# Matmul operands at many 16-byte steps modulo 256, and every second paired unit's products in halves of 256 tokens, in a two-layer encoder trunk

## The chip, the cores and the metric

The kernel runs on one core of a Trainium2 chip, in one launch. The metric is the device time of that core in microseconds: three runs of the kernel before, and one further execution taken by the hardware profiler.

## The reference

Two sequences of 512 tokens (prompt and sample), width 1024, pass through the same two layers with the same parameters. Layer 1 is differential attention with 8 heads, layer 2 bidirectional retention with 8 heads; each layer projects into a width of 2048, gates the mixer's output and projects back:

```python
def diff_attention(h, w_in, lq1, lk1, lq2, lk2, subln_g, w_out, lambda_init):
    proj = h @ w_in
    q, k, v, gate = jnp.split(proj, [DA_QK_WIDTH, 2 * DA_QK_WIDTH, 2 * DA_QK_WIDTH + D_INNER], axis=-1)
    ...  # rotary on q and k; per head two score maps, softmax, a = p0 - lam * p1, a @ v
    o = rms_norm(o, subln_g, SUBLN_EPS) * (1.0 - lambda_init)
    o = o.reshape(B, S, D_INNER) * jax.nn.silu(gate)
    return o @ w_out

def trunk(x, norm_g, ...):
    for i in range(DEPTH):            # DEPTH = 2
        h = rms_norm(x, norm_g[i], NORM_EPS)
        x = x + (diff_attention if i % 2 == 0 else bidir_retention)(h, ...)
    return rms_norm(x, final_norm_g, NORM_EPS)
```

All of it is float32. The matmuls read their operands as float32r, and a product is made of three: high part by high part, high by low, low by high.

## The kernel before

**Stages.** Input norm and the first projection; attention with its output projection; the second projection; retention with its output projection; the final norm. The two sequences are the two columns of a 2 x 2 block product, and each projection is done with seven block products (P1 to P7) in place of eight: the sums and differences of weight blocks are made for each unit, those of token blocks once for each layer.

**Token operands.** `make_b` writes, for each of seven names (B11, B21, T1, T2, B22, T3, T4) and four parts k of the contraction, a buffer `[128, 2, 512]`: high and low part of 512 tokens. `slot(n, ...)` gives each its place: 18 places in one large tile `arena`, and tiles of their own (`b12`, `b13`, `b20` to `b27`) for the others. The same places later hold q, k, v, the attention weights `aT` and the mixer's output `oT`. A place starts in the arena at `32 + at * 1024 + shift` elements of four bytes; `shift` is 0, 16 or 32 elements, so that the places stand at three steps of 64 bytes modulo 256.

**Units.** A `Unit` is 256 columns of an input projection. A *paired* unit (q, k or gate; 24 in layer 1 and 16 in layer 2) computes transposed: the weights are the stationary operand, 128 columns at a time, and 512 tokens are the moving operand, 12 matmuls for each product (4 parts by 3 passes, line 573). A *wide* unit (v; 4 in each layer) has the tokens stationary, 128 at a time, and 256 weight columns moving, 48 matmuls for each product (line 580). `prep` splits a product's weights into high and low parts in buffers `ws`, a ring of `WS_BUFS = 7`. `evac` empties the PSUM banks: `c` copies on ScalarE, sums into `e` on VectorE (line 610). The ring of `e` has 8 places.

**Other matmuls.** Line 1007 is attention's scores, line 1059 attention times v, line 1160 retention's scores, line 1178 retention times v, line 824 the output projection (`oT` stationary, `ws` moving), lines 755, 946 and 1043 transposes.

**Order.** Every operation is recorded with a cost and its dependencies in a `Plan`, which then lays them out engine by engine; a ring's place is taken again when all who used it are done. TensorE's operations keep the recorded order within a window of 24. A product of a paired unit is one operation of cost 2.79, whatever matmuls it issues.

Of the kernel before, what the change touches and what calls it, by code (L numbers as in the profile page):

```python
# [10 lines left out]
F32R = mybir.dt.float32r  # L11
# [4 lines left out]
P = 128  # L16
S = 512
D = 1024
KT = D // P
NT = S // P  # L20
# [10 lines left out]
PASSES = ((0, 0), (0, 1), (1, 0))  # L31
WS_BUFS = 7
# [208 lines left out]
def trunk_kernel(  # L241
# [7 lines left out]
    nc = tc.nc  # L249
    xs = (x_prompt, x_sample)  # L250
    ys = (y_prompt, y_sample)
    plan = Plan()

    sm = ctx.enter_context(tc.tile_pool(name="sm", bufs=1))
    cp = ctx.enter_context(tc.tile_pool(name="cp", bufs=1))
    ar = ctx.enter_context(tc.tile_pool(name="ar", bufs=1))
# [10 lines left out]
    def view(pool, tag, i, size, shape, dt=F32):  # L267


        if size % 16 and pool in (cp, wk):  # L270
            pool = sm
        if (tag, i) not in places:
            places[tag, i] = pool.tile([P, size], F32, tag=f"{tag}{i}", name=f"{tag}_{i}", bufs=1)
        n = math.prod(shape[1:])
        t = places[tag, i][0:shape[0], 0:n]
        if dt != F32:
            t = t.bitcast(dt)
        if len(shape) == 3:
            t = t.rearrange("p (a b) -> p a b", a=shape[1])
        elif len(shape) == 4:  # L280
            t = t.rearrange("p (a b c) -> p a b c", a=shape[1], b=shape[2])
        return t

    def work(tag, shape, bufs, dt=F32, name=None):
        size = SIZE.get(tag, shape[1])
        return Buf(plan, tag, bufs, lambda i: view(wk, tag, i, size, shape, dt))

    arena = ar.tile([P, 18 * 1024 + 80], F32R, tag="arena", name="arena")

    def slot(n, shape, dt=F32R, shift=0):  # L290

        size = math.prod(shape[1:])
        at = None if n in (12, 13) or n >= 20 else n if n < 12 else n - 2
        if at is None:
            assert not shift
            cnt[0] += 1
            label = f"b_{cnt[0]}"
            return Buf(plan, f"b{n}", 1, lambda i: cp.tile(shape, dt, tag=f"b{n}", name=label))  # L300
        assert dt == F32R
        lo = 32 + at * 1024 + shift

        def make(i):
            t = arena[:, lo:lo + size]
            return t.rearrange("p (a b) -> p a b", a=shape[1]) if len(shape) == 3 else t
        b = Buf(plan, f"b{n}", 1, make)
        b.also = Buf(plan, f"edge{at + 1 if shift else at}", 1, None)
        return b

    def const(shape, tag, dt=F32):
        return Buf(plan, tag, 1, lambda i: view(cp, tag, i, math.prod(shape[1:]), shape, dt))

    def ws_t(shape):
        return work("ws", shape, WS_BUFS, F32R)

    def raw_t(shape):
        return work("raw", shape, 4)
# [5 lines left out]
        return work("c", [P, S], 4, name=name)  # L324

    def e_t(name="e"):
        return work("e", [P, S], 8, name=name)

    def m_t(name="m"):
        return work("m", [P, S], 4, name=name)  # L330
# [9 lines left out]
    def bank(tag, name=None):  # L340
        return Buf(plan, tag, BUFS[tag], lambda i: view(pj if tag == "pj" else sc, tag, i, S, [P, S]))
# [31 lines left out]
    def pe(cost, fn, r, w):  # L373
        plan.op("PE", cost, fn, r, w)

    def dma(out, in_, r, w, kb, eng=None):

        q = eng or nc.sync
        plan.op("SP" if eng is None else "ACT", 0.5, lambda: q.dma_start(out(), in_()), r, w, lands=2.0 + kb / 200.0,
                kb=kb, load=any(isinstance(k[0] if isinstance(k, tuple) else k, Buf) for k in w))  # L380
# [109 lines left out]
            yield  # L490


    class Unit:
        def __init__(self, w, c0, kind, done, view=None):


            self.w, self.c0, self.kind, self.done = w, c0, kind, done
            self.view = view or (lambda r, i: r[:, :, i * P:(i + 1) * P])
            self.wide = kind == "wide"
            self.n_ws = 2 if self.wide else 1  # L500
            self.early = None
            self.ops, self.x, self.s = {}, {}, {}
            self.banks = {}

# [55 lines left out]
        def product(self, op):  # L560
            which = BANK_OF[op]
            n_banks = 2 if self.wide else 1
            opens = op in OPENS
            if opens:
                self.banks[which] = [bank(dict(x="pj", z="sc", y="o")[which], which) for _ in range(n_banks)]
            a, b = self.ops.pop(op), B_OF[op]
            bt = [Bop[b, k] for k in range(4)]
            reads = [q[1] for q in a] + bt

            def pair(ps):  # L570
                for k in range(4):
                    for i, (u, v) in enumerate(PASSES):
                        nc.tensor.matmul(  # L573
                            ps.t, a[u][0]()[:, k, :], bt[k][:, v, :], start=(opens and k == 0 and i == 0),
                            stop=(k == 3 and i == 2), skip_group_check=True)

            def wide(ps, t):
                for k in range(4):
                    for i, (u, v) in enumerate(PASSES):
                        nc.tensor.matmul(  # L580
                            ps[:, (t % 2) * 256:(t % 2) * 256 + 256], bt[k][:, v, t * P:(t + 1) * P],
                            a[u][0]()[:, k, :], start=(opens and t % 2 == 0 and k == 0 and i == 0),
                            stop=(k == 3 and i == 2), skip_group_check=True)

            if not self.wide:
                ps = self.banks[which][0]
                pe(2.79, lambda: pair(ps), reads, [ps])
                return
            for t in range(NT):
                ps = self.banks[which][t // 2]  # L590
                pe(1.43, lambda ps=ps, t=t: wide(ps, t), reads, [ps])
# [172 lines left out]
        lo_of(256, lambda: oT[1][:, :, tok], lambda: og.t, lambda: oT[0][:, :, tok], [og, (oT[0], t)], [(oT[1], t)])  # L764

    def new_oT(g):
        return [slot(16 + 2 * g + a, [P, 2, S], F32R, 32) for a in range(2)]

    def load_qk(src, i, shift):
        t = slot(i, [P, 2, S], F32R, shift)  # L770
        dma(lambda: t.t.bitcast(F32), lambda: src[0][src[1]], [src[0]], [t], 512)
        return t

    def load_v(src, i):
        out = []
        for a in range(2):
            t = slot(i + a, [P, NT, 256], F32R, 16)
            dma(lambda a=a, t=t: t.t.bitcast(F32), lambda a=a: src[a].rearrange("p (t e) -> p t e", t=NT),
                [src], [t], 512)
            out.append(t)  # L780
        return out

    def load_sg(src):
        t = os_t(F32, "sg")
        dma(lambda: t.t, lambda: src[:], [src], [t], 512)
        return t
# [68 lines left out]
    qk_d = {}  # L855
# [132 lines left out]
    qk, vt, sg, oT = {}, {}, {}, {}  # L988
    st = [{} for _ in tiles]

    def fetch1(h, g):
        for j in range(2):
            for which in range(2):
                qk[h, g, j, which] = load_qk((qk_d[0, which, h, g], j), 4 * which + 2 * g + j, 16 * which)
        vt[h, g] = load_v(v_d[0, h, g], 8 + 2 * g)
        sg[h, g] = load_sg(g_d[0, h, g])

# [39 lines left out]
    def transp(i):  # L1037
        p = st[i]['p']
        tp = bank("tp", "tpa")

        def fn():
            for j in range(NT):
                nc.tensor.transpose(tp[:, j * P:(j + 1) * P], p[:, 0, j * P:(j + 1) * P], ident.t)  # L1043
        pe(0.44, fn, [p, ident], [tp])
        aT = slot(14 + i % 2, [P, 2, S], F32R, 32)
        hi_of(S, lambda: aT[:, 0, :], lambda: tp.t, [tp], [(aT, 0)])
        lo_of(S, lambda: aT[:, 1, :], lambda: tp.t, lambda: aT[:, 0, :], [tp, (aT, 0)], [(aT, 1)])
        st[i]['aT'] = aT
# [76 lines left out]
    qk, vt, sg, oT = {}, {}, {}, {}  # L1125
    Fs, aTs, os_, ons = {}, {}, {}, {}

    def fetch2(b):
        h, g = blocks[b]
        for which in range(2):  # L1130
            qk[b, which] = load_qk((qk_d[1, which, h - h % 2, g], h % 2), 12 * which + b % 2, 16 - 16 * which)
        vt[b] = load_v(v_d[1, h, g], 2 + 2 * (b % 2))
        sg[b] = load_sg(g_d[1, h, g])

# [18 lines left out]
    def score2(b, j):  # L1153
        h, g = blocks[b]
        s = bank("sc", "s2")
        q, k = qk[b, 0], qk[b, 1]

        def fn():
            for i, (u, v) in enumerate(PASSES):
                nc.tensor.matmul(s.t, k[:, u, j * P:(j + 1) * P], q[:, v, :], start=(i == 0), stop=(i == 2))  # L1160
        pe(0.7, fn, [q, k], [s])
        t1 = e_t("rt")
        F = Fs[h]
        dve(S, lambda: nc.vector.tensor_tensor(t1.t, s.t, F[:, 384 - P * j:896 - P * j], op=ALU.mult), [s, F], [t1])
        aT = slot((6 + j, 10 + j if j < 2 else 12 + j)[b % 2], [P, 2, S], F32R, 32)
        hi_of(S, lambda: aT[:, 0, :], lambda: t1.t, [t1], [(aT, 0)])
        lo_of(S, lambda: aT[:, 1, :], lambda: t1.t, lambda: aT[:, 0, :], [t1, (aT, 0)], [(aT, 1)])
        aTs[b, j] = aT
# [41 lines left out]
    for i in range(N2 + 2):  # L1210
        if i < N2:
            b, t = tiles2[i]
# [9 lines left out]
        if 0 <= i - 1 < N2:  # L1222
            b1, t1 = tiles2[i - 1]
            h, g = blocks[b1]
# [60 lines left out]
```

## Time and profile before

| | |
|---|---|
| three runs | 1857.8, 1864.89, 1865.54 us |
| median | 1864.89 us |
| profiled execution, span from its first to its last instruction | 1856.5 us |
| TensorE busy (matmuls) | 1823.4 us, 10337 matmuls |
| VectorE busy | 1450.6 us |
| ScalarE busy | 926.7 us |
| DMA queue of the kernel's transfers | 305.45 MB, 48.6% of the 16 engines' time |

The profile gives its execution by the span alone. The trace's engines are PE (TensorE's matmuls), PEld (its weight loads), DVE (VectorE), ACT (ScalarE), POOL (GpSimd) and SP (the queue of DMA issues). A row of groups has the line of the program, engine, operation, `out<-in`, shapes and count, then busy us and the mean ns of one, then idle time before them. A row of the chain of waits has a start, a length in us, and the work done in it; pieces of the chain follow each other without a gap, so a piece's length over its count is the time from start to start.

### The profile page before, as it was taken

Reading aid. Unit: us, or ns where it says so; the run is one execution under the profiler, and the core shown is the slowest. Engines: PE = TensorE matmul, PEld = TensorE weight load, DVE = VectorE, ACT = ScalarE, POOL = GpSimd, SP = SyncE. Lnnn points to the kernel's source line nnn. Section 1 sums busy time; section 2 is a strip of 40 time slices with the busy share of each in tenths; the row PEclk is TensorE's granted clock in tenths of the full one; section 3 lists DMA queues with packets and bytes.
Section 4 is the critical chain, followed back from the end, with each engine's and each line's share of the span. In section 5 each row is a group of like instructions: output and inputs, shape, how many; then the busy total and the mean of one; then the engine's idle time right before and its main releaser. Section 6 shows DMA issues by size and latency. Waiting matters only on the chain.

```text
span 1856.5 us, 27778 instructions
## 1 busy us (share of the span) xinstructions
PE 1823.4 (98%) x10337; PEld 1578.6 (85%) x10337; DVE 1450.6 (78%) x2423; ACT 926.7 (50%) x1897; POOL 152.8 (8%) x372
## 2 busy tenths in 40 slices
PE   6999999999999999999999999999999999999998
PEld 5888988988988878888888888989898988888886
DVE  7979688688688588888888896777777767766777
ACT  6734444343344465555555874435353454444444
POOL 3000000000000011111111300000000001111112
PEclk9999999999999999999999999999999999999999
DMA  4335544545545774444453433553545487434542
GB/s 161 119 119 182 182 136 153 177 124 181 160 126 173 266 272 179 182 170 153 153 183 125 159 97 103 168 170 130 174 143 165 142 313 268 169 146 168 195 145 91
DMA packets 149696, 307.31 MB, mean 166 GB/s; under 512 B 11940, under 2 KB 71992, under 8 KB 149560
## 3 DMA queue, kind: packets, MB, share of 16 engines
q1 hardware_dynamic: 149376, 305.45, 48.6%
q8 instruction: 81, 1.33, 0.3%
q14 instruction: 55, 0.45, 0.1%
q10 hardware_dynamic: 184, 0.08, 0.0%
HBM read 196.43 MB, written 109.05 MB: 165 GB/s over the span
## 4 chain that ended last, share of the span: by engine, by line
PE 91%; DVE 4%; ACT 2%; issue 1%; DMA 1%; POOL 1%; POOLq 0%; DVEq 0%; ACTq 0%
PE pj L573 22%; PE pj L824 18%; PE sc L573 11%; PE pj L580 9%; PE o L573 5%; PE o L1059 5%; PE o L1178 5%; PE sc L580 5%; PE sc L1007 5%; PE o L580 2%; PE sc L1160 2%; PE o L755 1%; PE tp L1043 1%; DVE ws L386 1%; DMA raw<-in_da_w_out_dram 1%
## 5 line engine op out<-in xcount | busy, mean ns | idle before, releaser
L824 PE MATMUL pj<-ws,arena 128*128 128x512 f32 x1536 | 399.5, 397 | 0.0
L824 PEld LDWEIGHTS pj<-ws,arena 128*128 128x128 f32 x1536 | 278.9, 188 | 54.1
L573 PE MATMUL pj<-b,ws 128*128 128x512 f32 x1200 | 293.6, 391 | 0.6 <-DVE e L610 0.6
L573 PEld LDWEIGHTS pj<-b,ws 128*128 128x128 f32 x1200 | 224.7, 188 | 49.6 <-issue 1.0
L829 DVE TENSOR_TENSOR b<-pj,b 128x512 f32<-128x512 f32 x256 | 176.1, 688 | 108.1 <-PE pj L824 107.7
L573 PE MATMUL sc<-arena,ws 128*128 128x512 f32 x960 | 232.3, 392 | 1.9 <-DVE arena L441 1.9
L386 DVE TENSOR_TENSOR ws<-st,ws 128x512 fp32r<-128x512 f32 (+1 forms) x192 | 148.1, 776 | 92.7 <-ACT ws L383 58.4
L573 PEld LDWEIGHTS sc<-arena,ws 128*128 128x128 f32 x960 | 180.1, 188 | 41.4 <-DVE arena L441 2.1
L386 DVE TENSOR_TENSOR ws<-raw,ws 128x512 fp32r<-128x512 f32 (+1 forms) x172 | 147.2, 861 | 83.5 <-ACT ws L383 72.4
L383 ACT CAST ws<-st 128x512 fp32r<-128x512 f32 (+1 forms) x192 | 131.9, 693 | 100.1 <-PE pj L573 35.8
L573 PE MATMUL pj<-arena,ws 128*128 128x512 f32 x720 | 177.5, 392 | 0.2 <-DVE arena L386 0.2
L383 ACT CAST ws<-raw 128x512 fp32r<-128x512 f32 (+1 forms) x172 | 130.8, 766 | 75.6 <-PE o L573 45.4
L739 POOL TENSOR_SCALAR css<-css 128x1 f32<-128x1 f32 x128 | 33.7, 263 | 1631.6 <-ACT o L737 918.3
L573 PEld LDWEIGHTS pj<-arena,ws 128*128 128x128 f32 x720 | 134.6, 188 | 29.3 <-DVE arena L386 0.5
L602 ACT COPY c<-pj 128x512 f32<-128x512 f32 x112 | 65.2, 583 | 128.5 <-PE pj L573 78.6
L573 PE MATMUL o<-arena,ws 128*128 128x512 f32 x480 | 116.0, 392 | 3.0 <-DVE e L441 3.0
L580 PE MATMUL pj<-ws,b 128*128 128x256 f32 x960 | 116.8, 276 | 0.0
L580 PEld LDWEIGHTS pj<-ws,b 128*128 128x128 f32 x960 | 113.2, 188 | 0.7
L1023 ACT ACTIVATE b<-sc,nm 128x512 f32<-128x512 f32 x128 | 88.0, 687 | 50.6 <-DVE nm L1015 50.5
L573 PEld LDWEIGHTS o<-arena,ws 128*128 128x128 f32 x480 | 89.4, 188 | 22.3 <-ACT ws L383 3.0
L1059 PE MATMUL o<-arena 128*128 128x256 f32 x768 | 106.8, 289 | 0.0
L1007 PE MATMUL sc<-arena 128*128 128x512 f32 x384 | 100.6, 398 | 4.0 <-ACT b L1023 4.0
(162 smaller groups left out, 2896.8 us busy)
## 6 DMA issues: line engine op xcount, KB each, us to landing
qk<-os SPq DMA_DIRECT2D x192, 256.0 KB, 3.9
arena<-qk SPq DMA_DIRECT2D x80, 512.0 KB, 4.8
raw<-in_da_w_in_dram SPq DMA_DIRECT2D x64, 512.0 KB, 5.1
v<-os SPq DMA_DIRECT2D x64, 512.0 KB, 4.2
arena<-v SPq DMA_DIRECT2D x64, 512.0 KB, 4.4
raw<-in_ret_w_in_dram SPq DMA_DIRECT2D x48, 512.0 KB, 4.2
os<-g SPq DMA_DIRECT2D x32, 512.0 KB, 7.5
g<-e SPq DMA_DIRECT2D x48, 256.0 KB, 4.4
```

What stands on the lines that cost most here:

```text
L383: act(n, lambda: nc.scalar.copy(dst(), src()), r, w)
L386: dve(n, lambda: nc.vector.tensor_tensor(dst(), src(), hi().bitcast(F32), op=ALU.subtract), r, w)
L573: nc.tensor.matmul(ps.t, a[u][0]()[:, k, :], bt[k][:, v, :], start=(opens and k == 0 and i == 0), stop=(k == 3 and i == 2), skip_group_che ...
L580: nc.tensor.matmul(ps[:, (t % 2) * 256:(t % 2) * 256 + 256], bt[k][:, v, t * P:(t + 1) * P], a[u][0]()[:, k, :], start=(opens and t % 2 == ...
L602: act(S, lambda c=c, ps=ps: nc.scalar.copy(c.t, ps.t), [ps], [c])
L824: nc.tensor.matmul(ps.t, o[a][:, e, t * P:(t + 1) * P], u[b][:, e, :], start=(n == 0), stop=(n == 5))
L829: dve(S, lambda: nc.vector.tensor_tensor(half, ps.t, half, op=ALU.add), [ps, (x, i)], [(x, i)])
L1007: nc.tensor.matmul(s.t, q[:, a, t * P:(t + 1) * P], k[:, b, :], start=(n == 0), stop=(n == 2))
L1023: act(840, lambda j=j, s=s, m=m: nc.scalar.activation(p[:, j, :], s.t, AF.Exp, bias=m.t, accum_out=sm[:, j:j + 1]), [s, m], [(p, j), (sm, j)])
L1059: nc.tensor.matmul(o[:, 0:256], aT[:, a, j * P:(j + 1) * P], v[b][:, j, :], start=(n == 0), stop=(n == 11))
L1160: nc.tensor.matmul(s.t, k[:, u, j * P:(j + 1) * P], q[:, v, :], start=(i == 0), stop=(i == 2))
L1178: nc.tensor.matmul(o[:, 0:256], a_[j][:, u, t * P:(t + 1) * P], v_[v][:, j, :], start=(n == 0), stop=(n == 11))
```

## The change

There are two edits, and a third that makes room for them.

First, operands' places. The arena's 18 places are laid out by `skew(n)`, which puts them at 16 different steps of 16 bytes modulo 256; buffers outside the arena get 16 elements more and start `n % 4 * 4` elements in; and the seven `ws` buffers become parts of one tile `ws_all` at seven different steps. `shift` is gone from all callers.

Second, each unit counts itself (`nth`), and a paired unit with an odd number issues each product as two halves of 256 tokens: 24 matmuls that each load their weights, in place of 12.

Third, the ring of `e` has 7 places.

```diff
-    arena = ar.tile([P, 18 * 1024 + 80], F32R, tag="arena", name="arena")
-    def slot(n, shape, dt=F32R, shift=0):
+    def skew(n):
+        return n % 4 * 4 + n // 4 % 4 * 16
+    homes = [0]
+    for at in range(1, 18):
+        n = at if at < 12 else at + 2
+        lo = homes[-1] + 1024
+        homes.append(lo + (skew(n) - lo) % 64)
+    arena = ar.tile([P, homes[-1] + 1024], F32R, tag="arena", name="arena")
+    ws_home = [j * 1024 + skew_j for j, skew_j in enumerate((0, 8, 20, 40, 52, 80, 108))]
+    ws_all = ar.tile([P, ws_home[-1] + 1024], F32R, tag="ws_all", name="ws_all")
+    def slot(n, shape, dt=F32R):
...
-            return Buf(plan, f"b{n}", 1, lambda i: cp.tile(shape, dt, tag=f"b{n}", name=label))
+            def own(i):
+                t = cp.tile([P, 1040], dt, tag=f"b{n}", name=label)[:, n % 4 * 4:n % 4 * 4 + size]
+                return t.rearrange("p (a b) -> p a b", a=shape[1]) if len(shape) == 3 else t
+            return Buf(plan, f"b{n}", 1, own)
...
-        lo = 32 + at * 1024 + shift
         def make(i):
-            t = arena[:, lo:lo + size]
+            t = arena[:, homes[at]:homes[at] + size]
             return t.rearrange("p (a b) -> p a b", a=shape[1]) if len(shape) == 3 else t
-        b = Buf(plan, f"b{n}", 1, make)
-        b.also = Buf(plan, f"edge{at + 1 if shift else at}", 1, None)
-        return b
+        return Buf(plan, f"b{n}", 1, make)
...
     def ws_t(shape):
-        return work("ws", shape, WS_BUFS, F32R)
+        def make(i):
+            t = ws_all[:, ws_home[i]:ws_home[i] + 1024]
...
+        return Buf(plan, "ws", WS_BUFS, make)
...
-        return work("e", [P, S], 8, name=name)
+        return work("e", [P, S], 7, name=name)
...
+            self.nth = next(nth_unit)
...
             def pair(ps):
+                if self.nth % 2:
+                    for half in range(2):
+                        at = slice(half * 256, half * 256 + 256)
+                        for k in range(4):
+                            for i, (u, v) in enumerate(PASSES):
+                                nc.tensor.matmul(
+                                    ps[:, at], a[u][0]()[:, k, :], bt[k][:, v, at],
+                                    start=(opens and half == 0 and k == 0 and i == 0),
+                                    stop=(k == 3 and i == 2), skip_group_check=True)
+                    return
                 for k in range(4):
                     for i, (u, v) in enumerate(PASSES):
...
-        t = slot(i, [P, 2, S], F32R, shift)                       # load_qk; q 0 and k 16, or 16 and 0
+        t = slot(i, [P, 2, S], F32R)
...
-            t = slot(i + a, [P, NT, 256], F32R, 16)               # load_v
+            t = slot(i + a, [P, NT, 256], F32R)
...
-        aT = slot(14 + i % 2, [P, 2, S], F32R, 32)                # transp; likewise score2 and new_oT
+        aT = slot(14 + i % 2, [P, 2, S], F32R)
```

On TensorE, early in the first projection, two units' products P5 follow each other into the banks `sc` and then the third unit's and others' into `pj`; the operands are a token operand (`arena` or a `b` tile, moving) and weights (`ws`, stationary). Before:

```order
L573 MATMUL sc_297<-arena,ws_438 128x512 x12
L573 MATMUL sc_311<-arena,ws_278 128x512 x12
L573 MATMUL pj_349<-b_541,ws_284 128x512 x3
L573 MATMUL pj_349<-b_556,ws_284 128x512 x3
L573 MATMUL pj_349<-arena,ws_284 128x512 x6
L573 MATMUL pj_375<-b_541,ws_364 128x512 x3
L573 MATMUL pj_375<-b_556,ws_364 128x512 x3
```

The same place after, where line 601 is the old line 573 and line 594 the new one, and all weights lie in `ws_all`:

```order
L601 MATMUL sc_296<-arena,ws_all 128x512 x12
L594 MATMUL sc_310<-arena,ws_all 128x256 x24
L601 MATMUL pj_348<-b_559,ws_all 128x512 x3
L601 MATMUL pj_348<-b_574,ws_all 128x512 x3
L601 MATMUL pj_348<-arena,ws_all 128x512 x6
L594 MATMUL pj_373<-b_559,ws_all 128x256 x3
L594 MATMUL pj_373<-b_574,ws_all 128x256 x3
```

The products stand in the same order; of two units that alternate, one is whole and the other in halves. The halves of one product go through all four parts of the token operand twice.

On VectorE, where these products' banks are emptied (line 610 before, 638 after, is a bank plus a copy into `e`; 386 and 401 write a low part; 636 and 664 multiply by a rotary table), before:

```order
L386 TENSOR_TENSOR ws_419<-st_393,ws_419 128x512
L636 SCALAR_TENSOR_TENSOR e_683<-e_683,cos_1046 128x512
L610 TENSOR_TENSOR e_440<-pj_375,c_431 128x512
L386 TENSOR_TENSOR os_302<-m_372,os_302 128x512
L386 TENSOR_TENSOR ws_421<-st_399,ws_421 128x512
L636 SCALAR_TENSOR_TENSOR m_335<-e_509,cos_1046 128x512
```

and after:

```order
L401 TENSOR_TENSOR ws_all<-st_403,ws_all 128x512
L664 SCALAR_TENSOR_TENSOR e_779<-e_779,cos_1147 128x512
L401 TENSOR_TENSOR os_301<-m_370,os_301 128x512
L638 TENSOR_TENSOR e_508<-pj_373,c_438 128x512
L401 TENSOR_TENSOR ws_all<-st_409,ws_all 128x512
L664 SCALAR_TENSOR_TENSOR m_334<-e_718,cos_1147 128x512
```

The sum that empties the bank `pj` stands one instruction later than before, behind a low part of a finished block.

More of the change, by code (lines that the diff above doesn't have):

```diff
@@ L296, in slot @@
         if at is None:
-            assert not shift
             cnt[0] += 1
             label = f"b_{cnt[0]}"
-            return Buf(plan, f"b{n}", 1, lambda i: cp.tile(shape, dt, tag=f"b{n}", name=label))
+            def own(i):
+                t = cp.tile([P, 1040], dt, tag=f"b{n}", name=label)[:, n % 4 * 4:n % 4 * 4 + size]
+                return t.rearrange("p (a b) -> p a b", a=shape[1]) if len(shape) == 3 else t
+            return Buf(plan, f"b{n}", 1, own)
         assert dt == F32R
-        lo = 32 + at * 1024 + shift
         def make(i):
-            t = arena[:, lo:lo + size]
+            t = arena[:, homes[at]:homes[at] + size]
             return t.rearrange("p (a b) -> p a b", a=shape[1]) if len(shape) == 3 else t
-        b = Buf(plan, f"b{n}", 1, make)
-        b.also = Buf(plan, f"edge{at + 1 if shift else at}", 1, None)
-        return b
+        return Buf(plan, f"b{n}", 1, make)
     def const(shape, tag, dt=F32):
@@ L314, in ws_t @@
     def ws_t(shape):
-        return work("ws", shape, WS_BUFS, F32R)
+        def make(i):
+            t = ws_all[:, ws_home[i]:ws_home[i] + 1024]
+            if len(shape) == 3:
+                return t.rearrange("p (a b) -> p a b", a=shape[1])
+            return t.rearrange("p (a b c) -> p a b c", a=shape[1], b=shape[2])
+        return Buf(plan, "ws", WS_BUFS, make)
     def raw_t(shape):
@@ L490, in make_b @@
             yield
+    nth_unit = itertools.count()
     class Unit:
@@ L766, in new_oT, with load_qk @@
     def new_oT(g):
-        return [slot(16 + 2 * g + a, [P, 2, S], F32R, 32) for a in range(2)]
-    def load_qk(src, i, shift):
-        t = slot(i, [P, 2, S], F32R, shift)
+        return [slot(16 + 2 * g + a, [P, 2, S], F32R) for a in range(2)]
+    def load_qk(src, i):
+        t = slot(i, [P, 2, S], F32R)
         dma(lambda: t.t.bitcast(F32), lambda: src[0][src[1]], [src[0]], [t], 512)
@@ L993, in fetch1 @@
             for which in range(2):
-                qk[h, g, j, which] = load_qk((qk_d[0, which, h, g], j), 4 * which + 2 * g + j, 16 * which)
+                qk[h, g, j, which] = load_qk((qk_d[0, which, h, g], j), 4 * which + 2 * g + j)
         vt[h, g] = load_v(v_d[0, h, g], 8 + 2 * g)
@@ L1130, in fetch2 @@
         for which in range(2):
-            qk[b, which] = load_qk((qk_d[1, which, h - h % 2, g], h % 2), 12 * which + b % 2, 16 - 16 * which)
+            qk[b, which] = load_qk((qk_d[1, which, h - h % 2, g], h % 2), 12 * which + b % 2)
         vt[b] = load_v(v_d[1, h, g], 2 + 2 * (b % 2))
@@ L1164, in score2 @@
         dve(S, lambda: nc.vector.tensor_tensor(t1.t, s.t, F[:, 384 - P * j:896 - P * j], op=ALU.mult), [s, F], [t1])
-        aT = slot((6 + j, 10 + j if j < 2 else 12 + j)[b % 2], [P, 2, S], F32R, 32)
+        aT = slot((6 + j, 10 + j if j < 2 else 12 + j)[b % 2], [P, 2, S], F32R)
         hi_of(S, lambda: aT[:, 0, :], lambda: t1.t, [t1], [(aT, 0)])
```

## The prediction, made before the result was known

> **What bounds the kernel now.** I read the page's head first, for the engine that sets the end.
>
> ```profile
> span 1856.5 us, 27778 instructions
> PE 1823.4 (98%) x10337; PEld 1578.6 (85%) x10337; DVE 1450.6 (78%) x2423; ACT 926.7 (50%) x1897; POOL 152.8 (8%) x372
> PEclk9999999999999999999999999999999999999999
> PE 91%; DVE 4%; ACT 2%; issue 1%; DMA 1%; POOL 1%; POOLq 0%; DVEq 0%; ACTq 0%
> ```
>
> PE is busy 98% of the span, at an undisturbed clock, and carries 91% of the chain that ended last. So the kernel is as long as its stream of matmuls, and a change is worth what it does to the time from one matmul's start to the next. PE's table of waits says how often the stream stops.
>
> ```profile
> PE tp L403 <- DMA on<-in_ret_subln_g_dram: 6.6, 1, 6.6
> PE sc L1007 <- ACT b L1023: 4.0, 1, 4.0
> PE o L573 <- DVE e L441: 3.0, 2, 2.8
> PE pj L573 <- DVE e L610: 0.6, 1, 0.6
> ```
>
> These are the longest entries and the one that concerns the ring of e buffers: a few us in all, at starts of stages. The stream itself is left, and the mean durations of the groups do not show its pace, because each has a pipeline's tail in it. The chain does show it: its pieces run from start to start. First a stretch of the first projection.
>
> ```profile
> 409.04 8.24 PE pj L573 x36
> ...
> 313.20 2.75 PE pj L573 x12
> 315.95 5.47 PE pj L580 x48
> 321.42 2.75 PE pj L573 x12
> 324.16 5.47 PE o L580 x48
> 329.63 5.44 PE sc L580 x48
> 335.07 5.44 PE pj L580 x48
> ```
>
> A paired unit's matmul over 512 tokens (L573) takes 8.24 us / 36 = 228.9 ns. A wide unit's matmul over 256 columns (L580) takes 5.44 / 48 = 113.3 ns once it has run for a while; the 48 that come right after an L573 product take 5.47. Two of them, 226.7 ns, are thus a little cheaper than one matmul of 512 columns, although they load weights twice. Then attention and, in the last row, retention.
>
> ```profile
> 660.36 1.38 PE o L1059 x12
> ...
> 805.12 1.42 PE o L1059 x12
> 806.54 1.38 PE sc L1007 x6
> 807.92 1.38 PE pj L824 x6
> ...
> 814.15 1.38 PE pj L824 x6
> 815.53 0.44 PE tp L1043 x4
> 815.97 1.39 PE pj L824 x6
> ...
> 1602.86 1.42 PE o L1178 x12
> ```
>
> Here 256 columns cost 1.42 / 12 = 118.3 ns, in the second layer as in the first, yet the same line at 660.36 did it in 1.38 / 12 = 115.0, with its operands at the same steps modulo 256 as later. A matmul of 512 columns costs 1.38 to 1.39 / 6, some 230.8 ns. So one shape has at least two paces, 113.3 and 118.3, and the same address residues can show more than one. That is what I go by: the pace depends on how a matmul's read and the next weights' load fall against each other, and on what ran just before.
>
> How many there are of each stands in the groups by shape:
>
> ```profile
> L824 PE MATMUL pj<-ws,arena 128*128 128x512 f32 x1536 | 399.5, 397 | 0.0
> L573 PE MATMUL pj<-b,ws 128*128 128x512 f32 x1200 | 293.6, 391 | 0.6 <-DVE e L610 0.6
> L573 PE MATMUL sc<-arena,ws 128*128 128x512 f32 x960 | 232.3, 392 | 1.9 <-DVE arena L441 1.9
> L573 PE MATMUL pj<-arena,ws 128*128 128x512 f32 x720 | 177.5, 392 | 0.2 <-DVE arena L386 0.2
> L580 PE MATMUL pj<-ws,b 128*128 128x256 f32 x960 | 116.8, 276 | 0.0
> L573 PE MATMUL o<-arena,ws 128*128 128x512 f32 x480 | 116.0, 392 | 3.0 <-DVE e L441 3.0
> L1059 PE MATMUL o<-arena 128*128 128x256 f32 x768 | 106.8, 289 | 0.0
> L1178 PE MATMUL o<-arena 128*128 128x256 f32 x768 | 100.9, 281 | 0.0
> L1007 PE MATMUL sc<-arena 128*128 128x512 f32 x384 | 100.6, 398 | 4.0 <-ACT b L1023 4.0
> L580 PE MATMUL sc<-ws,arena 128*128 128x256 f32 x768 | 89.6, 276 | 0.0
> L580 PE MATMUL pj<-ws,arena 128*128 128x256 f32 x576 | 72.0, 276 | 0.0
> L1160 PE MATMUL sc<-arena,b 128*128 128x512 f32 x192 | 58.9, 417 | 0.6 <-DVE e L1164 0.6
> L580 PE MATMUL o<-ws,arena 128*128 128x256 f32 x384 | 45.0, 277 | 0.0
> ```
>
> L573 has 3360 matmuls, L580 2688, L824, L1007 and L1160 together 2112, L1059 and L1178 together 1536.
>
> **The change part by part. Halves.** Of the 40 paired units every second one, so 20 x 7 products x 12 = 1680 of L573's matmuls, becomes 3360 of 256 columns, and as many weight loads are added. Nothing hides this: all of it lies on PE. At the pace of the settled row, two halves cost 226.7 ns, 2.2 less than one whole: 1680 x 2.2 = 3.7 us gained. At the pace of L1059's row they cost 236.6: 1680 x 7.7 = 12.9 us lost. Which pace it is hangs on the addresses, and the second half of the change moves those too.
>
> **Addresses.** Before, in the built program, every moving and every stationary operand of lines 573, 580, 824, 1007, 1059, 1160 and 1178 starts at one of 32, 96, 160 and 224 bytes modulo 256, and the two of one matmul always differ by 64 or 192. After, the paired products meet all 16 differences in steps of 16 bytes (of the 1680 matmuls that stay whole, each difference has between 18 and 231), the wide ones too, and within one product the place changes with each of the four parts of the token operand, so after every third matmul. The trace has no operand at another step than those four, so this cost can only be bounded. What speaks for a cost: L580 reaches 113.3 only after a run at fixed steps, and right behind other addresses 48 of them take 0.03 us more; after the change the steps shift every third matmul, so the settled pace should be met less often. I therefore put every 256-column matmul of the projections two thirds of the way from 113.3 to 118.3, at 116.6 ns, since 118.3 is the row of those that come in short runs between other work. That gives:
>
> - halves: 1680 x (2 x 116.6 - 228.9) = 1680 x 4.3 = 7.2 us lost (ends: 3.7 gained, 12.9 lost);
> - wide units: 2688 x (116.6 - 113.3) = 8.9 us lost (ends: 0 and 2688 x 5.0 = 13.4);
> - the 1680 that stay whole: between 228.9 and the 231.7 of the slower L824 row (1.39 / 6), I take 230.5: 1680 x 1.6 = 2.7 us lost (ends: 1680 x 2.2 = 3.7 gained, if they fall to 226.7, and 4.7 lost);
> - L824, L1007, L1160, L1059 and L1178: they already stand at the slow ends of these pairs, nothing is taken (ends: 2112 x 4.1 = 8.7 and 1536 x 5.0 = 7.7 gained; the loss is priced under the rivals).
>
> **A rule against this.** The Trainium skill says otherwise on the page "TensorE: Matmul & The Clock Gate", section "Step-by-step: what each phase is for": TensorE has two independent read ports into SBUF, and loading the next weights takes no bandwidth from the running matmul. Its section "Back-to-back issue gap" gives N / 2.4 + 2.5 ns, an estimate of 215.8 ns for 512 columns and 109.2 for 256. By that page addresses would be worth nothing and the halves 1680 x 2.6 = 4.4 us lost, an estimate; the rows above are 13 and 4 to 9 ns over its figures and vary at one shape, so the trace does not bear it out in full.
>
> **One e buffer fewer, and order.** Seven places instead of eight move some 50 of DVE's 2400 instructions by one to a few places, and about a dozen each on ACT and SP; PE's products keep their order. The sums that go through e empty a PSUM bank, and PE waits for them in the 0.6 us and 3.0 us rows above only.
>
> ```profile
> 30.00:480.00 450.00, 444.75 (x2414) 383.27 (x2413) 370.23 (x569) 210.09 (x354) 0.00 (x0) 1.00 0.47 144
> L379 SPq DMA_DIRECT2D g<-e x48: 319/428/1574, 55.3 to 1522.3; - x48
> ```
>
> The first row is a stretch of the first projection (PE, PEld, DVE, ACT and POOL busy in it): DVE has 80 of 450 us free there, which covers an instruction that comes one place later. I cost it at nothing. Without the cover a gate's store from an e buffer (48 of them, second row) holds up the next sum on DVE, the bank behind it and then PE. Loads and stores start at other steps as well, but the DMA share of 0.47 leaves them room; nothing for that.
>
> The sum is 7.2 + 8.9 + 2.7 = 18.8 us. The profiled execution is known by its span, 1856.5 us; 1856.5 + 18.8 = 1875.3. The three runs have their median at 1864.89, 8.4 above that span, and the forecast for the median is 1884 us, 1.0% slower. Its own range goes from 1874 to 1896: the upper end is 12.9 + 13.4 + 4.7 = 31.0 us, the lower the limit of what can be told, since 0.5% (9.3 us) is about what a measurement of this kernel can tell from no change.
>
> **The rivals.**
>
> *Addresses do nothing; only the halves count.* For it: 8.24 for 36 and 2.75 for 12 repeat all through the projection, whatever DVE, ACT and DMA do beside it, and 113.3 is L580's pace over thousands of matmuls. Against it: 1.38 and 1.42 for the same 12. The time: 1864.9 - 3.7 = 1861, no change. Chance 0.2. It is the rule of the page above, with the halves priced by the trace.
>
> *The new steps pull the two reads apart*, so that every 512 columns cost 226.7 and every 256 cost 113.3. For it: 113.3 is a pace that PE holds with a weight load under every matmul, so the loads alone do not prevent it. Against it: nothing in the new places favours the good differences over the others. The gain is 3.7 (halves) + 3.7 (whole ones) + 8.7 + 7.7 = 23.8 us: 1841, faster by 1.3%. It decides as soon as the mean over 256 columns falls below about 113.5 in the halves and the attention lines together. Chance 0.2.
>
> *Some differences are much worse than any in the trace*: the extra 5.0 ns of the slow pace comes twice per matmul. Then 256 columns cost 123.3 in the projections: 1680 x 17.7 = 29.7 and 2688 x 10.0 = 26.9 us; 5 ns more on the other 1680 + 2112 + 1536 matmuls add 26.6. Together 83 us, 1948; at half of that 1906. For it: 16 differences hold more extremes than two. Against it: the four steps in the trace, at distances of 64 and of 192, lie within 5.0 ns of each other. Chance 0.1.
>
> *The shorter e ring stops PE*: at each of the 16 gate units a wait like the two of L573 on e (3.0 us for 2, so 1.5 each), 24 us, 1889. Against it: DVE's free 80 us. Chance 0.05.
>
> **How the numbers follow.** The forecast has 0.45. Slower by over 0.5%: 0.45 + 0.1 + 0.05 = 0.6; within 0.5%: 0.2; faster by over 0.5%: 0.2. The range 1840 to 1915 us holds the forecast, the no-change case, the e ring, the upper half of the faster case and the lowest part of the worst one, about 0.8.
>
> **What would show each step.** In the chain of the new profile, 24 halves in a row at 2.80 us (116.6 each) and 48 wide ones at 5.60 would be the forecast; 2.72 and 5.44 the no-change case; 12 whole ones near 2.77. Pieces of one line should now differ from product to product, as the steps do. PE's waits should stay under 30 us with e no longer than before. I am wrong if the halves cost less than 114.4 each (they then gain), if the attention lines move by more than 3 ns, or if the span changes while the pieces of the chain do not.

## The result, and the profile after

The changed kernel takes 1891.18 us (median of 4 runs, 1889.2 to 1892.81) against 1862.99 us (median of 4, 1857.8 to 1865.54) for the kernel before: a ratio of 1.0157, 95% interval 1.0135 to 1.018. It is slower by 1.6%; the forecast was 1884 us and 1.0%. Paces and sums below are read from the one profiled execution of each kernel.

The head of the page after, with the same rows as before:

```profile
span 1891.0 us, 31145 instructions
PE 1858.6 (98%) x12017; PEld 1674.8 (89%) x12017; DVE 1452.0 (77%) x2423; ACT 929.9 (49%) x1897; POOL 151.3 (8%) x372
PEclk9999999999999999999999999999999999999999
PE 93%; ACT 2%; DMA 2%; DVE 1%; POOL 1%; issue 1%; SPq 0%; POOLq 0%; DVEq 0%; ACTq 0%
```

The 1680 further matmuls are there (12017 against 10337), DVE and ACT are as busy as before, the clock is the same, and PE still carries the chain. The span grew by 34.5 us, PE's busy time by 35.2. The time lies in the stream of matmuls, and the chain after, in the first projection and in attention, shows where (start, length, work; the pieces run from start to start):

```profile
281.12 8.35 PE pj L601 x36
...
311.75 2.84 PE sc L594 x24
314.60 2.85 PE pj L594 x24
...
323.13 5.67 PE pj L608 x48
...
331.62 5.69 PE o L608 x48
...
399.28 8.48 PE pj L594 x72
...
803.22 1.40 PE pj L852 x6
804.83 1.42 PE o L1087 x12
```

Halves (L594) cost 8.48 / 72 = 117.8 ns to 2.85 / 24 = 118.8 ns, two of them 235.6 to 237.5, where one whole matmul cost 228.9. Wide ones (L608) went from 113.3 to 5.67 / 48 = 118.1, whole ones (L601) from 228.9 to 8.35 / 36 = 231.9, the output projection (L852) from 1.38 or 1.39 to 1.40 for 6. Attention times v (L1087) stayed at 1.42 for 12. Summed from start to start over all matmuls of a line, before and after:

| lines (before) | us before | us after | difference |
|---|---|---|---|
| 573, paired units | 771.0 | 789.4 | +18.4 |
| 580, wide units | 305.2 | 317.5 | +12.3 |
| 824, output projection | 361.5 | 363.3 | +1.8 |
| 1007 and 1160, scores | 141.2 | 143.2 | +2.0 |
| 1059 and 1178, times v | 187.1 | 188.5 | +1.4 |
| transposes | 75.3 | 74.2 | -1.1 |

That is the whole difference: 34.8 us by these sums, 34.5 by the spans. PE's waits on e are no longer than they were, 4.2 us in all before and after:

```profile
PE o L601 <- DVE e L456: 2.8, 1, 2.8
PE sc L1188 <- DVE e L1192: 1.4, 2, 1.1
```

### The profile page after: what moved, and what is told of

Same layout as the page of the kernel before. It is cut to its first block, busy times and chain, and to the rows that moved or that the text cites. A ratio compares the mean times of both kernels' runs of the same rounds, so it can differ in the third digit from the quotient of the medians.

```text
span 1891.0 us, 31145 instructions
## 1 busy us (share of the span) xinstructions
PE 1858.6 (98%) x12017; PEld 1674.8 (89%) x12017; DVE 1452.0 (77%) x2423; ACT 929.9 (49%) x1897; POOL 151.3 (8%) x372
## 3 DMA queue, kind: packets, MB, share of 16 engines
q1 hardware_dynamic: 149376, 305.45, 47.7%
## 4 chain that ended last, share of the span: by engine, by line
PE 93%; ACT 2%; DMA 2%; DVE 1%; POOL 1%; issue 1%; SPq 0%; POOLq 0%; DVEq 0%; ACTq 0%
PE pj L852 17%; PE pj L601 11%; PE pj L594 11%; PE pj L608 10%; PE sc L601 6%; PE sc L594 6%; PE sc L608 5%; PE o L1087 5%; PE o L1206 5%; PE sc L1035 4%; PE o L601 3%; PE o L594 3%; PE o L608 2%; PE sc L1188 2%; PE tp L1071 1%; PE o L783 1%
## 5 line engine op out<-in xcount | busy, mean ns | idle before, releaser
L852 PE MATMUL pj<-ws_all,arena 128*128 128x512 f32 x1536 | 402.1, 398 | 0.0
L852 PEld LDWEIGHTS pj<-ws_all,arena 128*128 128x128 f32 x1536 | 279.1, 188 | 56.3
L401 DVE TENSOR_TENSOR ws_all<-st,ws_all 128x512 fp32r<-128x512 f32 (+1 forms) x192 | 148.0, 775 | 103.7 <-ACT ws_all L398 64.2
L401 DVE TENSOR_TENSOR ws_all<-raw,ws_all 128x512 fp32r<-128x512 f32 (+1 forms) x172 | 147.2, 860 | 89.7 <-ACT ws_all L398 73.3
L398 ACT CAST ws_all<-st 128x512 fp32r<-128x512 f32 (+1 forms) x192 | 132.1, 693 | 122.0 <-PE pj L601 29.5
L398 ACT CAST ws_all<-raw 128x512 fp32r<-128x512 f32 (+1 forms) x172 | 130.9, 766 | 87.8 <-PE o L594 33.1
L594 PE MATMUL pj<-b,ws_all 128*128 128x256 f32 x1200 | 154.6, 281 | 0.0
L594 PEld LDWEIGHTS pj<-b,ws_all 128*128 128x128 f32 x1200 | 148.2, 188 | 1.4 <-ACT c L630 0.2
L601 PE MATMUL pj<-b,ws_all 128*128 128x512 f32 x600 | 148.5, 394 | 0.1
L601 PEld LDWEIGHTS pj<-b,ws_all 128*128 128x128 f32 x600 | 111.3, 188 | 25.4 <-issue 0.5
L608 PE MATMUL pj<-ws_all,b 128*128 128x256 f32 x960 | 121.1, 280 | 0.0
L594 PE MATMUL sc<-arena,ws_all 128*128 128x256 f32 x960 | 120.1, 281 | 0.0
L601 PE MATMUL sc<-arena,ws_all 128*128 128x512 f32 x480 | 117.7, 394 | 1.2 <-DVE arena L456 1.2
L608 PEld LDWEIGHTS pj<-ws_all,b 128*128 128x128 f32 x960 | 117.1, 188 | 0.5
L594 PEld LDWEIGHTS sc<-arena,ws_all 128*128 128x128 f32 x960 | 116.7, 188 | 0.4
L601 PEld LDWEIGHTS sc<-arena,ws_all 128*128 128x128 f32 x480 | 89.6, 188 | 21.6 <-DVE arena L456 1.5
L1087 PE MATMUL o<-arena 128*128 128x256 f32 x768 | 107.8, 290 | 0.0
```

What stands on the lines that cost most here:

```text
L398: act(n, lambda: nc.scalar.copy(dst(), src()), r, w)
L401: dve(n, lambda: nc.vector.tensor_tensor(dst(), src(), hi().bitcast(F32), op=ALU.subtract), r, w)
L594: nc.tensor.matmul(ps[:, at], a[u][0]()[:, k, :], bt[k][:, v, at], start=(opens and half == 0 and k == 0 and i == 0), stop=(k == 3 and i = ...
L601: nc.tensor.matmul(ps.t, a[u][0]()[:, k, :], bt[k][:, v, :], start=(opens and k == 0 and i == 0), stop=(k == 3 and i == 2), skip_group_che ...
L608: nc.tensor.matmul(ps[:, (t % 2) * 256:(t % 2) * 256 + 256], bt[k][:, v, t * P:(t + 1) * P], a[u][0]()[:, k, :], start=(opens and t % 2 == ...
L852: nc.tensor.matmul(ps.t, o[a][:, e, t * P:(t + 1) * P], u[b][:, e, :], start=(n == 0), stop=(n == 5))
```

## The experiments

All start from the kernel before unless it says otherwise. "Difference" is the moving operand's start less the stationary one's, modulo 256 bytes, by the addresses in the built program; before, it is 64 in paired units and the output projection and 192 in wide units and the products with v.

**Halves alone.** Only the second edit; places and e as before.

```diff
+                if self.nth % 2:
+                    for half in range(2): ...   # 24 matmuls of 256 tokens
```

> The kernel before with the second edit alone: every second paired unit in halves, all places and the ring of e as before. Settling theory (a pace of 113.3 ns for 256 columns is reached only while operands' steps modulo 256 stay the same from matmul to matmul, whatever the steps are): steps are constant here, so halves run at 113 to 114 ns, 24 in 2.72 us, wide ones stay at 113.3 and whole ones at 228.9; the kernel gains 3 to 4 us, 0.2%. Rival, halves themselves are slow (weights loaded twice as often hold up the stream): halves at 117 to 119, 24 in 2.83, a loss of 11 to 13 us, and the wide ones unchanged.

Measured: 1861.73 us, ratio 1.0008, 0.9994 to 1.0022. The chain at two places (L579 halves, L586 whole, L593 wide):

```profile
140.39 2.83 PE pj L579 x24
143.22 2.76 PE pj L586 x12
...
179.45 2.83 PE pj L579 x24
182.28 5.46 PE pj L593 x48
187.73 2.72 PE pj L579 x24
190.45 5.65 PE o L593 x48
...
407.59 2.72 PE sc L579 x24
```

Both theories are half right. Halves of one shape, at one difference, take 2.72 us (113.3 ns each) in one product and 2.83 (117.9) in the next; of the 140 products in halves 80 run at 113 and 60 at 118, and none in between. The wide ones do the same here: 5.46, then 5.65. So 256 columns at the old differences have two steady paces, and a product keeps the one that it began with. Nor is the pace drawn anew for each product; it is handed on, as the lines from 179.45 on show: slow halves, a fast wide product, fast halves, a slow wide product. In this run and in the one with all paired units in halves, taken together, halves right behind halves keep the pace 338 times out of 341, a wide product right behind halves has the other pace 37 times out of 38, and halves right behind a wide product have its pace 34 times out of 34. Weights that are loaded twice as often do not slow the stream by themselves, and the halves alone neither gain nor lose what can be measured.

**The steps alone.** The changed kernel with every paired unit whole.

```diff
-                if self.nth % 2:
+                if False:
```

> The changed kernel with all paired units whole: the 16-byte steps and seven e buffers alone. Settling theory: whole ones 231.8 ns (12 in 2.78 us), so 3360 x 2.9 = 10 us, wide ones 118.2, so 2688 x 4.9 = 13 us, and 3 to 5 us on the other lines: 26 to 28 us slower than before. Rival, it is the halves that unsettle the rest: whole ones near 229.5 and wide ones near 114, 3 to 6 us slower than before.

Measured: 1881.56 us, ratio 1.0116, 1.0093 to 1.0139. The chain (L601 whole, L608 wide):

```profile
313.80 2.76 PE pj L601 x12
316.56 2.77 PE sc L601 x12
319.33 2.78 PE pj L601 x12
322.11 5.67 PE pj L608 x48
327.78 2.80 PE pj L601 x12
```

The 16-byte steps alone bring the wide ones to 118.1 and the whole ones to 230 to 233.3, and with them 1.2 of the 1.6%. The halves add the rest: two of them cost 236.3 ns on the mean in the changed kernel where a whole one costs 231.9, 1680 x 4.4 = 7.4 us. That it is the halves that unsettle the others is out.

**All ws buffers 16 bytes further on**, the same in every matmul, with the seven buffers in one tile:

```diff
-        return work("ws", shape, WS_BUFS, F32R)
+        lo = i * 1024 + 4                       # elements of four bytes, in ws_all
```

> The kernel before with one edit: all seven ws buffers 16 bytes further on, so that paired matmuls differ by 48 and wide ones by 208 modulo 256 in place of 64 and 192, the same in every matmul. Settling theory: the steps are new but constant, so wide ones settle at 113.3 and whole ones at 228.9, and the time stays within 3 us of before. Step theory (a start off the old 32 modulo 64, or a difference other than 64 and 192, costs by itself): wide ones 118, whole ones 232, and a loss of 13 + 10 = 23 us, with about 2 us on the output projection.

Measured: 1881.54 us, ratio 1.011, 1.0086 to 1.0133. The chain (L582 whole, L589 wide):

```profile
318.04 2.78 PE pj L582 x12
320.83 5.72 PE pj L589 x48
326.55 2.77 PE pj L582 x12
329.32 5.72 PE o L589 x48
```

This run decides against the reason that the prediction gave. The steps never change here, and yet wide ones cost 119.2 and whole ones 231: as much as with steps that change all the time. A steady difference does not help if it is a slow one.

**Buffers at the four old steps, but different ones.** The seven ws buffers 64 bytes apart modulo 256:

```diff
+        lo = i * 1024 + i * 16
```

> The kernel before with one edit: the seven ws buffers stand 64 bytes apart modulo 256, so all operands keep the four old steps, but which one changes from buffer to buffer. In a wide product the high and the low part lie in two buffers and alternate within every three matmuls; in a paired product both lie in one and the difference stays the same for 12. Settling theory: wide ones near 118, 13 us slower; whole ones between 229 and 231, 0 to 6 us; in all 10 to 20 us slower. Step theory (16-byte positions cost, multiples of 64 do not): wide ones 113.3 and whole ones 229, the time within 3 us of before. Difference theory (64 and 192 are good, 0 and 128 bad, however steady): about half of the way, and then paired products with a difference of 0 or 128 stand out by some ns against those with 64 and 192.

Measured: 1873.74 us, ratio 1.0074, 1.0049 to 1.0098. The chain (L582 whole, L589 wide); the differences of the five whole products are 0, 192, 128, 64 and 0, in this order:

```profile
305.63 2.74 PE o L582 x12
308.37 2.80 PE sc L582 x12
311.17 2.79 PE pj L582 x12
313.96 2.75 PE sc L582 x12
316.71 2.73 PE pj L582 x12
319.45 5.65 PE pj L589 x48
```

For whole products the difference alone says the pace: 2.73 to 2.74 us at 0, 2.75 at 64, 2.79 at 128, 2.80 at 192. 0 is not bad, as the difference theory had it, but the best. Wide products, whose high and low parts now lie in buffers of different steps, run at 117.7 (36 of 56) to 121.0 ns and never at 113.3. Whether it is the change from matmul to matmul that takes the fast pace away, as settling says, this run does not show: three of the four differences mixed here give wide ones 117.7 to 120.0 in the runs below without any change, and at the fourth, 192, they can run at 118 too.

**Everything 32 bytes further on**, by an unused tile in front; all differences stay.

```diff
+    sm.tile([P, 8], F32, tag="pad", name="pad")
```

> The kernel before with one edit: an unused 32-byte tile ahead of everything, so that every buffer starts 32 bytes further on, at 0, 64, 128 and 192 modulo 256 in place of 32, 96, 160 and 224; all differences stay as they were. Difference theory (the pace follows from how far the moving operand and the weights are apart modulo 256, and from whether that stays): whole ones 228.9, wide ones 113 to 114, the time within 3 us of before. Position theory (the old 32 modulo 64 is what matters): whole ones near 232 and wide ones near 118, about 20 us slower.

Measured: 1860.64 us, ratio 0.9999, 0.9985 to 1.0014. The chain (L574 whole, L581 wide):

```profile
315.66 2.75 PE pj L574 x12
318.40 5.66 PE pj L581 x48
324.06 2.77 PE pj L574 x12
...
1178.11 5.47 PE pj L581 x48
1183.58 2.75 PE pj L574 x12
1186.32 5.47 PE o L581 x48
1191.79 5.44 PE sc L581 x48
```

The positions themselves cost nothing that the time shows. Whole ones keep 229. The wide ones take both paces without any change of difference: all 28 products of layer 1 are at 117.8, as in the first three lines, and all 28 of layer 2 at 113.3 to 114, as in the others. The traces, read matmul by matmul, show what goes with it. Whole ones at a difference of 64 are not even: they repeat about 226, 229 and 232 ns in turn. Where the step from the last whole matmul to the first wide one takes 226 or 227 ns, the wide product is slow, and where it takes 230 or more, it is fast; that holds for all 106 such crossings in the traces of before, of the halves alone, of this run, of seven places for e and of paired at 0 with wide at 192, 36 of them slow and 70 fast. The two go together; that the step is the cause is not shown.

**ws 32 and 64 bytes further on**, to see how the steady pace follows the difference (`+ 8` and `+ 16` elements).

> The kernel before with one edit: all ws buffers 32 bytes further on; paired matmuls differ by 32 and wide ones by 224, the same in every matmul. Difference theory: a difference between 0 (paired products of the mixed run settled at 226.5 there) and 48 (231.9), so whole ones at 227 to 232; wide ones near 119 as at 208; 8 to 20 us slower. Settling theory: constant steps, so 228.9 and 113.3, within 3 us of before; it has failed at 48 already, and falls for good if this run is slower by more than 5 us.

> The kernel before with one edit: all ws buffers 64 bytes further on; paired and wide matmuls have a difference of 0 in every matmul, the output projection 128. Difference theory, from the mixed run, where paired products at 0 settled at 226.5 and wide ones have no settled row at 0: whole ones 226.5 to 227, a gain of 3360 x 2.2 = 7 us; wide ones between 113.3 and 118, 0 to 13 us lost; the output projection 0 to 3 us lost; in all 1855 to 1870. Bank theory (two reads that start at the same place modulo 256 collide): whole ones above 232, wide ones above 118, over 20 us slower.

Measured: 1885.74 us, ratio 1.0145 (1.0129 to 1.0162), and 1870.25 us, ratio 1.0057 (1.004 to 1.0073). The chain of the first:

```profile
103.65 8.40 PE pj L582 x36
...
322.60 5.68 PE pj L589 x48
```

and of the second:

```profile
102.59 8.16 PE pj L582 x36
...
331.31 5.76 PE sc L589 x48
```

At a difference of 32 whole ones cost 233.3 ns, as much as at any tried, and wide ones (224) 118.3. At 0 whole ones cost 226.7, less than before, and wide ones 120.0, as much as at any steady one: the best difference for one shape is among the worst for the other. Two reads that start at the same place do not simply collide.

**Seven places for e.**

```diff
-        return work("e", [P, S], 8, name=name)
+        return work("e", [P, S], 7, name=name)
```

> The kernel before with one edit: 7 places for e in place of 8. The prediction's term: nothing, the time within 2 us of before, the pace of every line unchanged, TensorE's waits on e under 4 us. Rival: at each of the 16 gate units a wait of about 1.5 us, 24 us slower.

Measured: 1858.53 us, ratio 0.9992, 0.9973 to 1.001: nothing, as costed.

**Towards a faster one.** Paired units at 0 and wide ones at 192, then at 64, then at 128; the ring of e with 7 places makes the room.

```diff
+        lo = i * 1088 + (16 if len(shape) == 4 else 0)     # wide at 192; for 64 and 128 wide ones get 32 and 48
```

> The kernel before with the two best steady differences together: a ws buffer used by a paired unit starts 64 bytes further on than one used by a wide unit or the output projection, so paired matmuls have a difference of 0, wide ones 192 and the output projection 64 as before; 7 places for e make the room. Difference theory: whole ones 226.9, wide ones 113.3 where they lock and 118 where they do not, the output projection 230.2 as before; 3360 x 2.0 = 6.7 us gained, 0.36%, and less if the wide ones now enter in the slower state. Rival, which buffer is taken changes and with it how the runs enter: wide ones at 118, 2688 x 4.7 = 12.6 us lost, net 6 us slower.

> As the last combination (paired matmuls at a difference of 0, seven e buffers), with the wide ones at a steady 64 in place of 192. Lock theory: whole ones 226.8; the wide ones have a steady pace of their own at 64, not known yet: at 113.3 the kernel gains 6 to 7 us (0.35%), at 118 it loses 6, at 120 it loses 11. Mirror rival (64 and 192 are the same distance, so the same two paces, with the entry deciding): 113.3 or 118, nothing else.

> The same with the wide ones at a steady 128. Whole ones 226.8. Difference theory: paired products at 128 were slow in the mixed run (232.5), so wide ones at 118 to 121, 6 to 14 us slower than before. Rival, the farthest distance modulo 256 is the best: 113.3 steadily, 6 to 7 us faster.

Measured: ratios 1.002 (1.0006 to 1.0033), 1.0023 (1.0008 to 1.0039) and 1.0047 (1.0031 to 1.0063). The chain of the first (L582 whole, L589 wide):

```profile
321.97 2.72 PE pj L582 x12
324.69 5.65 PE o L589 x48
330.34 5.65 PE sc L589 x48
```

of the second:

```profile
330.67 5.65 PE sc L589 x48
```

and of the third:

```profile
329.58 5.76 PE sc L589 x48
```

The paired units give their gain, 226.7 ns, but all 56 wide products of the first run are at 118, where all 56 of the profile before run at 113, at the same difference. That fits the crossings above: whole ones at 0 take 226 or 227 ns each (3187 of 3360), without the turns of 229 and 232, and all 24 crossings are of the slow kind. 3360 x 2.2 = 7.4 us gained and 2688 x 4.4 = 11.8 lost. At 64 the wide ones cost 117.7 too, at 128 120. No version beat the kernel before by anything that can be measured.

**All paired units in halves**, at the old places.

```diff
+                if True:                                   # in place of: if self.nth % 2
```

> The kernel before with all 40 paired units in halves, at the old places. Lock theory (256 columns at the old differences have two steady paces, 113.3 and 118, and the way a run begins decides): no whole product comes between, so a stretch keeps one pace for long; between 3360 x 2.2 = 7 us faster and 3360 x 7 + 2688 x 4.7 = 36 us slower, and pieces of the chain at 2.72 or 2.83 for 24, few between. Rival, the pace is a mixture by chance from matmul to matmul: pieces spread between 2.72 and 2.83.

Measured: 1873.54 us, ratio 1.0071, 1.0043 to 1.0099. The chain (L579 halves, L593 wide):

```profile
314.84 2.83 PE sc L579 x24
317.66 2.83 PE pj L579 x24
320.49 5.45 PE pj L593 x48
325.94 2.72 PE pj L579 x24
```

Of 280 products 87 run at 113 and 193 at 118, by the median step of each. The two paces are what there is; the mixture by chance is out, and so is chance from product to product: long stretches keep one pace, and a wide product between halves turns it as told above. 6720 matmuls are exposed to it here, and the slow pace has more of them.

## Why the prediction was right, and what of it was not

**What bounds the kernel**: as read. The sum of starts explains the whole change. PE's waits on e are the same 4.2 us, DVE and ACT are busy 1.4 and 3.2 us more, and the DMA queue's share went from 48.6 to 47.7%.

**Halves, 7.2 us lost**: the sign was right and the size too small. Both ends of the step were real paces, 113.3 and 118.3, but the choice between them was made wrong: not two thirds of the way, but all of it. Two halves cost 236.3 in place of 233.2, 1680 x 7.4 = 12.4 us. The gain of 3.7 us that the settled row promised is there only for products in the fast pace, 80 of 140 in the run with the halves alone.

**Wide units, 8.9 us lost**: 12.3, by the same mis-sized step, 118.1 in place of 116.6; **whole ones, 2.7 us**: 231.9 in place of 230.5, so 1680 x 3.0 = 5.0. These three terms were each taken short of their upper ends and came out near them; their sum is 30 us in place of 18.8, and the upper ends gave 31.0. **The other lines, nothing**: about 4 us, most of it on the output projection and the scores.

**The reason.** The prediction said that steady steps give the fast pace and changing ones spoil it. The first half is wrong: at a steady 208 or 224 wide ones cost 119.2 and 118.3, and at the old, steady 192 they can run at 118. The second half is not shown. In the profile after, a wide matmul whose successor has the same difference takes 117.8 ns on the mean and one whose successor has another 118.4; for halves it is 118.2 and 117.9, for whole ones 231.6 and 232.0. So a change by itself is worth little there. What the new places did was to leave the two differences, 64 and 192, that alone of those tried let 256 columns run at 113.3, for a spread over all 16, at which 256 columns cost 118 on the mean and 512 cost 232. That the steady pace follows from the difference was in none of the steps. The 0.03 us that the prediction took as a sign of settling is in the trace some five matmuls of 116 to 123 ns behind a whole product, before 113 to 114: an entry, for which the wide ones' new shape is as good a reason as their new addresses.

**The rivals.** Addresses are not indifferent: the steps alone cost 1.2%. The rule of the Trainium skill, page "TensorE: Matmul & The Clock Gate", section "Step-by-step: what each phase is for", that weight loads take nothing from the running matmul, would make addresses worth nothing and is not borne out by this: moving ws alone by 16 bytes costs 1.1%, moving both operands together by 32 bytes nothing (0.9999). By which way the two operands hold each other up, no run shows. Reads pulled apart to 113.3 and 226.7 everywhere did not come; each pace exists, but not at one difference of those tried. The much worse differences do not exist among those tried, since nothing steady went over 120.0 and 233.3. The e ring cost nothing.

**The base.** The forecast was set 8.4 us above the profile's span, at the median. That 1884 came so near 1891.18 is in part luck: the terms were 15.7 us short, 18.8 for 34.5 between the spans, and the 8.4 us made up half of it, though the changed kernel's median lies only 0.2 above its own span of 1891.0. What makes the base move may be the two paces: the program that differs only by 32 bytes had half of its wide ones at 117.8 in a profile of 1861.5 us, and the profile before had all of them at 113.3 in 1856.5. Which pace the executions without a profile had is not known.

## To carry to other kernels

Where matmuls follow each other without a gap, read the chain's pieces from start to start, by shape, and compare equal pieces: a few ns apart is a property of the operands' places or of how the run began, and it multiplies by thousands. Choose places by the difference between moving operand and weights, measure that difference for each shape by itself, and expect that what ran just before goes with the pace that a run keeps; a spread over many differences cost 118 and 232 ns here where good ones cost 113.3 and 226.7 to 228.9, so a kernel that stands on a good one loses by it. A gain per matmul that is smaller than the distance between two paces of the same shape is not safe until both have been seen.

## What the runs showed of the hardware

- The steady time of one matmul, weights loaded each time, by difference. Moving 512 columns: 226.7 ns at 0, 233.3 at 32, 231.9 at 48, 228.9 at 64; in runs of 12 at 128 and 192, 232.5 and 233.3 (2.79 and 2.80 / 12). Moving 256 columns: 120.0 at 0, 117.7 at 64 after whole products at 0, 120.0 at 128, 113.3 or 118 at 192 and, in halves, at 64, 119.2 at 208, 118.3 at 224.
- At the same operands and the same difference, 256 columns have two steady paces, 113.3 and 118 ns, and a product of 24 or 48 matmuls stays in the one in which it began. It goes with the matmuls just before: halves and wide products right behind one another hand it on by a fixed rule (37 of 38 and 34 of 34), and behind whole ones a last step of 226 or 227 ns goes with the slow pace, one of 230 or more with the fast (106 of 106). Why was not found.
- Moving all operands together by 32 bytes changes nothing that the time shows (0.9999, 0.9985 to 1.0014), and whole matmuls keep 229 ns.
- Why a difference is good for 512 columns and bad for 256 stays open; no run here takes weight loads and matmuls apart.
